# Two-block encoder on one core: moving operands of the split matmuls laid at set distances from the weight buffers, and attention matmuls on full 128x128 tiles

## The chip, the cores and the metric

The kernel runs on one core of a Trainium2 chip. The metric is the device time of one execution in microseconds (us): 1568.88 us before the change, the median of 3 runs (1568.62 to 1571.0).

## The reference

Two blocks run over 256 tokens of width 1024. The first puts 16 meta tokens ahead (272 rows) and has an even layer (latent attention and windowed attention, 8 heads each) and an odd layer (a linear recurrence). The second has two layers of FFN, hybrid mixer, FFN. What matters here, cut from the source:

```
# latent attention: the rotary key is one for all heads, 64 wide; scores over 128 + 64
k_pe = jnp.broadcast_to(k_pe[:, None], (B, MLA_HEADS, T, MLA_ROPE))
k = jnp.concatenate([k_nope, k_pe], axis=-1)
q = rms_norm(q, g_qn); k = rms_norm(k, g_kn)      # per head, over 192
o = blocked_dense_attention(q, k, v, MLA_QK ** -0.5)
...
def swiglu(x, w_gate, w_up, w_down):
    return (jax.nn.silu(x @ w_gate) * (x @ w_up)) @ w_down     # 1024 -> 2816 -> 1024
...
for l in range(DEPTH):
    x = x + 0.5 * swiglu(rmsnorm(x, ffn1_norm[l]), ffn1_w_gate[l], ffn1_w_up[l], ffn1_w_down[l])
    h = rmsnorm(x, mix_norm[l])
    x = x + hybrid_mixer(h, w_in[l], ...)          # 1024 -> 4608, a 4-head gated memory, 1024 -> 1024
    x = x + 0.5 * swiglu(rmsnorm(x, ffn2_norm[l]), ffn2_w_gate[l], ffn2_w_up[l], ffn2_w_down[l])
```

## The kernel before

Activations lie transposed: features on the 128 partitions, tokens along the free axis. A large product is exact to fp32 by parts: weight w and activation x are each cut into a high part in fp32r (ACT, a copy) and a low part (DVE, a subtraction), and `prod` (L437) issues three matmuls for each 128 x 128 piece of weight: hi with xh, hi with xl, lo with xh. The weight is the stationary operand, the activation the moving one, 272 columns in the even layer and the first half of the odd one, 256 in the rest. `mm3` (L453) does the same for operands that are given one by one, `split` (L464) cuts an activation into its two parts, and `feed` (L484) does so for the next stage's x.

Raw weights come by DMA on the SP queue into two buffers; pieces of 1024 columns are cut from them into 4 pairs of buffers, hi0 to hi3 and lo0 to lo3 (`cut`, L418). `more_cuts` (L1400) adds a fifth pair, hi4 and lo4, for the odd layer and all after it. A piece is released by the last matmul that reads it (`used`).

The order of instructions is made by a planner in `Builder`: each call runs a cost model of the engines (`Clock`, L118), `tick` (L324) resumes side work (norms, gates, attention heads, written as generators) when the model says that its inputs are there, and `pump` (L393) cuts the next piece of weight. All instructions go through one helper, so that the profile gives nearly all of them line 179.

The stages, by their time in the trace: the even layer to about 300 us, the odd layer to about 480, then for each of the two layers ffn1 (480 to 665, 1020 to 1207), hybrid (665 to 845, 1207 to 1390) and ffn2 (845 to 1020, 1390 to 1567).

- FFN (`ffn`, L1327): for each of 22 slices of 128 hidden features, gate and up take 2 x 8 x 3 matmuls over x's 8 parts of 128 features (x moving, 1056 in an FFN); down takes 8 x 22 x 3 = 528 with the hidden features ph/pl moving.
- Hybrid (`hybrid`, L1442): 768 matmuls with x as stated above (`pair`, L1465), 384 with the parts hh/hl, hph/hpl and mh/ml of later products moving. `memory` has a helper `small` (L1524) that issues 32 matmuls of 32 x 32 in two bursts with a yield between, six times a layer, and at its end spreads one row of scales over 128 partitions from tiles of 4 partitions (`spread`, L458).
- Odd layer: its output product moves oyh/oyl; there DVE runs the recurrence.
- Even layer: `rowsum` (L681) adds squares over partitions into row j of a bank by a matmul with a 128 x 32 window of constants, 28 times; `head` (L861) spreads a row of key scales (`rowkh`, `rowkl`, 32 partitions, times a column of the 32 x 32 identity `identr`) and makes the scores of a latent head from two products for each half of the queries: `mq` with `mk` over 128 features, and `mqr` with `kpe` over 64 partitions (two heads share a 128-partition tile of `mqr`). `query_scales` (L737), `window_scales` (L798) and `latent_scales` (L827) work on 32 rows; `shared_key` (L690) makes `kpe`.

x's parts xh and xl are tiles [128, 8, 272]. FFN and hybrid use `[:, k, :256]` of them, so that part k begins 1088 bytes behind part k-1.

Of the kernel before, what the change touches and what calls it, by code (L numbers as in the profile page):

```python
# [16 lines left out]
P = 128  # L17
# [24 lines left out]
_CST = (("ident", 128), ("ones", 128), ("row", 63), ("pair", 64), ("pe", 32), ("hsel", 128), ("dsel", 16))  # L42
# [13 lines left out]
C_AT, C_N = _offsets(_CST)  # L56
R_AT, R_N = _offsets(_ROT)
# [167 lines left out]
class Builder:  # L225

    AHEAD = 3

# [26 lines left out]
    def t(self, pool, shape, tag, dt=F32):  # L255
        tile_ = pool.tile(shape, dt, tag=tag, name=tag)
        self.clock.read[tile_.tensor.name] = [(0, 1 << 30, self.clock.at["pe"] + 0.3)]
        return tile_

# [198 lines left out]
    def spread(self, out, p, r, hi, lo):  # L458

        row = self.identr[0:p, r:r + 1].to_broadcast([p, P])  # L460
        self.mm(out=out, lhsT=row, rhs=hi, start=True, stop=False)
        self.mm(out=out, lhsT=row, rhs=lo, start=False, stop=True)
# [21 lines left out]
    def feed(self, gen, d, x, g, n):  # L484
        self.split(x, self.xh[:, d, :n], self.xl[:, d, :n], g)
        self.put("x", gen, d)
        self.spawn(self.square(gen, d, x, n))

# [53 lines left out]
    def first_norm(self):  # L542
        yield from self.until(self.clock.known(self.clock.wrote, self.cst.tensor.name))
        self.act(out=self.identr, in_=self.c("ident")[0:32, 0:32], func=AF.Copy)
# [18 lines left out]
    def setup(self):  # L563
# [7 lines left out]
        self.identr = self.t(self.const, [32, 32], "identr", F32R)  # L571
# [9 lines left out]
    def even(self):  # L581
# [152 lines left out]
        rowk = self.t(ev, [32, T], "rowk")  # L734
        rowkh, rowkl = self.t(ev, [32, T], "rowkh", F32R), self.t(ev, [32, T], "rowkl", F32R)

        def query_scales(rows, c0):  # L737
# [10 lines left out]
            tt(out=pk, in0=cp[:, 64:80], in1=self.c("dsel"), op=ALU.mult)  # L748
# [41 lines left out]
        r1 = self.t(ea, [32, T], "r1")  # L790
        qmr = self.t(ea, [P, 4, P], "qmr")
        sel = self.t(ea, [32, P], "sel")
# [5 lines left out]
        def window_scales():  # L798
# [4 lines left out]
            sd, r2 = yield from some(2)  # L803
            tt(out=r1, in0=rows[0:32, :T], in1=rb[0:32, :], op=ALU.mult)
            tt(out=r1, in0=r1, in1=rb[0:32, :], op=ALU.mult)
            yield
            yield from inverse(r1, 1.0 / P, sd[0:32, :], r2[0:32, :])
            stt(out=r1, in0=r2[0:32, :], scalar=float(P) ** -0.5, in1=rb[0:32, :], op0=ALU.mult, op1=ALU.mult)
# [4 lines left out]
            self.drop(sd, r2, rows)  # L813
# [13 lines left out]
        def latent_scales():  # L827
            rows = sums["lrows"]
            self.own(rows)
            sd, r2 = yield from some(2)  # L830
            yield from inverse(rows[0:32, :T], 1.0 / 192, sd[0:32, :], rowk)
# [4 lines left out]
            self.drop(sd, r2, rows)  # L836
# [24 lines left out]
        def head(h):  # L861
# [72 lines left out]
        def latent_query(h, ps):  # L934
# [392 lines left out]
    def ffn(self, name, layer, gen, nxt):  # L1327
# [114 lines left out]
    def hybrid(self, layer, gen):  # L1442
# [43 lines left out]
        def memory():  # L1486
# [37 lines left out]
            def small(i, ls, rs):  # L1524
                for h in range(H):
# [5 lines left out]
                    if h == 1:  # L1531
                        yield
# [20 lines left out]
            yield from small(0, kk_, qs)  # L1553
            inc, up = lf, None
            for i in range(8):
# [18 lines left out]
                if i < 5:  # L1574
                    yield from small(i + 1, kq, kq)
# [52 lines left out]
            rrh, rrl = hh[0:H, H - 1, :], hl[0:H, H - 1, :]  # L1628
            self.split(tp[0:H, 0:S], rrh, rrl)
# [233 lines left out]
def _layout(i):  # L1863
# [29 lines left out]
    for l in range(2):  # L1893
# [30 lines left out]
    row, pair, pe = (np.zeros((P, n), f32) for n in (63, 64, 32))  # L1924
    row[:, 31] = 1.0
    pair[:64, 31] = 1.0
    pair[64:, 32] = 1.0
    pe[:64, 8:16] = 1.0
# [3 lines left out]
        "ident": np.eye(P, dtype=f32), "ones": np.ones((P, P), f32), "row": row, "pair": pair, "pe": pe, "hsel": hsel,  # L1932
# [49 lines left out]
```

## Time and profile before

| what | value |
|---|---|
| median of 3 runs | 1568.88 us |
| profiled execution, its own time | 1568.53 us |
| its span, first to last instruction | 1566.7 us |
| PE busy in the span | 1546.1 us |
| DVE busy | 1116.8 us |
| ACT busy | 904.5 us |
| POOL busy | 24.1 us |
| mean granted TensorE clock | 0.999 |

Times of matmuls in a row overlap: a recorded duration includes the pipeline, and what one costs in a stream is the distance from its start to the next start. An fp32 matmul (not fp32r) leaves two records. The chain of waits follows the work that ended last backwards, so a long piece of it with one engine and a count gives the time of that many matmuls in a row. The view by stretch gives the busy time of every engine in a piece of the span.

### The profile page before, as it was taken

Reading aid. Unit: us, or ns where it says so; the run is one execution under the profiler, and the core shown is the slowest. Engines: PE = TensorE matmul, PEld = TensorE weight load, DVE = VectorE, ACT = ScalarE, POOL = GpSimd, SP = SyncE. Lnnn points to the kernel's source line nnn. Section 1 sums busy time; section 2 is a strip of 40 time slices with the busy share of each in tenths; the row PEclk is TensorE's granted clock in tenths of the full one; section 3 lists DMA queues with packets and bytes.
Section 4 is the critical chain, followed back from the end, with each engine's and each line's share of the span. In section 5 each row is a group of like instructions: output and inputs, shape, how many; then the busy total and the mean of one; then the engine's idle time right before and its main releaser. Section 6 shows DMA issues by size and latency. Waiting matters only on the chain.

```text
span 1566.7 us, 31037 instructions
## 1 busy us (share of the span) xinstructions
PE 1546.1 (99%) x12950; PEld 1484.6 (95%) x12950; DVE 1116.8 (71%) x1882; ACT 904.5 (58%) x1435; POOL 24.1 (2%) x58
## 2 busy tenths in 40 slices
PE   8999999999999999999999999999999999999998
PEld 8897679999989999999999999999999999999998
DVE  6877665679997666669776666666666698777754
ACT  7667544589966554475455544445444755555443
POOL 0000000000000000000000000000000000000000
PEclk9999999999999999999999999999999999999999
DMA  6422223554354555654445654655555543556553
GB/s 231 157 88 82 81 70 119 192 173 154 135 185 169 207 181 169 207 179 138 162 160 189 215 180 163 201 184 191 181 173 201 179 161 127 174 185 215 172 167 120
DMA packets 42492, 259.20 MB, mean 165 GB/s; under 512 B 4840, under 2 KB 6128, under 8 KB 18416
## 3 DMA queue, kind: packets, MB, share of 16 engines
q1 hardware_dynamic: 40624, 251.98, 46.6%
q10 hardware_dynamic: 1728, 5.24, 1.0%
q8 instruction: 101, 1.65, 0.4%
q14 instruction: 39, 0.32, 0.1%
HBM read 256.16 MB, written 1.05 MB: 164 GB/s over the span
## 4 chain that ended last, share of the span: by engine, by line
PE 90%; DVE 6%; ACT 2%; issue 1%; DMA 1%; POOL 0%; POOLq 0%; ACTq 0%; SPq 0%; DVEq 0%
PE acc L179 66%; PE m L179 24%; DVE lo L179 2%; DVE big L179 1%; ACT hi L179 1%; DVE kq L179 1%; DVE work L179 0%; DVE xx L179 0%; ACT st L179 0%; DMA raw<-in_hin_dram 0%; DVE st L179 0%; POOL col L179 0%; DMA raw<-in_first_dram 0%; DVE pr L179 0%; DVE xc L179 0%
## 5 line engine op out<-in xcount | busy, mean ns | idle before, releaser
L179 DVE TENSOR_TENSOR lo<-raw,hi 128x1024 fp32r<-128x1024 f32 (+3 forms) x520 | 582.3, 1129 | 263.0 <-ACT hi L179 248.5
L179 ACT ACTIVATE hi<-raw 128x1024 fp32r<-128x1024 f32 (+3 forms) x520 | 502.3, 979 | 323.5 <-PE acc L179 206.6
L179 PE MATMUL acc<-xh,hi 128*128 128x256 f32 (+1 forms) x2088 | 591.7, 283 | 5.6 <-ACT hi L179 5.6
L179 PE MATMUL acc<-xl,hi 128*128 128x256 f32 (+1 forms) x2088 | 594.6, 285 | 0.0
L179 PE MATMUL acc<-xh,lo 128*128 128x256 f32 (+1 forms) x2088 | 593.2, 284 | 0.0
L179 PEld LDWEIGHTS acc<-xh,hi 128*128 128x128 f32 x2088 | 394.7, 189 | 9.4 <-ACT hi L179 5.6
L179 PEld LDWEIGHTS acc<-xh,lo 128*128 128x128 f32 x2088 | 395.1, 189 | 2.7 <-issue 1.4
L179 PEld LDWEIGHTS acc<-xl,hi 128*128 128x128 f32 x2088 | 393.4, 188 | 2.3
L179 PE MATMUL acc<-ph,hi 128*128 128x256 f32 x704 | 196.8, 279 | 0.0
L179 PE MATMUL acc<-ph,lo 128*128 128x256 f32 x704 | 196.7, 279 | 0.0
L179 PE MATMUL acc<-pl,hi 128*128 128x256 f32 x704 | 196.7, 279 | 0.0
L179 PEld LDWEIGHTS acc<-pl,hi 128*128 128x128 f32 x704 | 132.4, 188 | 0.0
L179 PEld LDWEIGHTS acc<-ph,lo 128*128 128x128 f32 x704 | 132.3, 188 | 0.0
L179 PEld LDWEIGHTS acc<-ph,hi 128*128 128x128 f32 x704 | 132.3, 188 | 0.0
L179 PE MATMUL m<-xh,lo 128*128 128x256 f32 (+1 forms) x344 | 99.0, 288 | 0.0
L179 PE MATMUL m<-xh,hi 128*128 128x256 f32 (+1 forms) x344 | 98.7, 287 | 0.0
L179 PE MATMUL m<-xl,hi 128*128 128x256 f32 (+1 forms) x344 | 98.7, 287 | 0.0
L179 DVE TENSOR_TENSOR work<-acc,spread 128x256 f32<-128x256 f32 (+1 forms) x107 | 45.5, 426 | 46.6 <-PE acc L179 46.4
L179 ACT ACTIVATE work<-work 128x256 f32<-128x256 f32 (+2 forms) x92 | 37.4, 408 | 54.9 <-DVE work L179 54.5
L179 PEld LDWEIGHTS m<-xh,lo 128*128 128x128 f32 x344 | 65.4, 190 | 1.4 <-issue 0.9
L179 PEld LDWEIGHTS m<-xl,hi 128*128 128x128 f32 x344 | 65.4, 190 | 0.9 <-issue 0.9
L179 PEld LDWEIGHTS m<-xh,hi 128*128 128x128 f32 x344 | 65.4, 190 | 0.6 <-issue 0.4
(361 smaller groups left out, 2230.7 us busy)
## 6 DMA issues: line engine op xcount, KB each, us to landing
raw<-in_ffn_gu_dram SPq DMA_DIRECT2D x88, 1024.0 KB, 4.9
raw<-in_ffn_dn_dram SPq DMA_DIRECT2D x64, 704.0 KB, 4.1
raw<-in_hin_dram SPq DMA_DIRECT2D x32, 1024.0 KB, 4.9
raw<-in_oin_dram SPq DMA_DIRECT2D x16, 1024.0 KB, 4.9
raw<-in_ein_dram SPq DMA_DIRECT2D x12, 1024.0 KB, 4.7
raw<-in_eout_dram SPq DMA_DIRECT2D x8, 1024.0 KB, 4.9
raw<-in_oout_dram SPq DMA_DIRECT2D x8, 1024.0 KB, 5.0
raw<-in_wph_dram SPq DMA_DIRECT2D x8, 1024.0 KB, 4.8
```

What stands on the lines that cost most here:

```text
L179: r = f(*args, **kw)
```

## The change

1. **Where moving operands lie.** If n is 256, `feed` now writes x's parts to `sh` and `sl`: views of the same tiles from 128 bytes on, with the 8 parts of 256 columns one behind the other (step 1024 bytes). `ffn` and `hybrid` read these. `ffn` puts a gap of 160 bytes, `hybrid` one of 32, ahead of its tiles; the constants' tile has become 636 bytes shorter. By the two programs' allocations, the distance of a matmul's moving operand from its weight piece, in bytes modulo 256 (a weight piece's own address is 128 modulo 256, but for hi4 and lo4 before, which are 0):

| moving operand (256 columns) | matmuls | distance before | distance after |
|---|---|---|---|
| x in FFN and hybrid | 5760 | 0, 64, 128, 192 by part k | 192 |
| ph, pl of the FFN | 2112 | 32 (160 with hi4, lo4) | 64 |
| hh, hl, hph, hpl, mh, ml of the hybrid | 768 | 32 (160 with hi4, lo4) | 192 |
| oyh, oyl of the odd layer | 384 | 64 (192 with hi4, lo4) | 192 |
| x in the odd layer's gate | 384 | 0, 64, 128, 192 | 0, 64, 128, 192 |

Operands of 272 columns keep all four distances.

2. **Full tiles.** Constants for `rowsum` come from a 405 column tile `pick` that POOL fills, and are 128 x 128 windows. `kpe` is copied by POOL into `kz`, one slice for even heads with the lower half zero and one for odd heads with the upper half zero, so that the score products take 128 partitions. `rowk`, `rowkh`, `rowkl`, `sel`, `kpe_sq`, `identr` have 128 partitions, and `query_scales` transposes 128 x 128 blocks. At the hybrid's end, `rc` is a zeroed tile of 256 columns, so that transposes and spreads are 128 x 128 too.

3. **`small`** has no yield within: its two bursts of 16 become one of 32.

The diff, cut to its core:

```diff
     AHEAD = 3
+    X_AT = 32
+    gaps = 0
...
+    def gap(self, pool, n):
+
+        if n:
+            self.gaps += 1
+            pool.tile([P, n // 4], F32, tag=f"gap{self.gaps}", name=f"gap{self.gaps}")
...
-    def spread(self, out, p, r, hi, lo):
-
-        row = self.identr[0:p, r:r + 1].to_broadcast([p, P])
+    def spread(self, out, r, hi, lo):
+
+        row = self.identr[:, r:r + 1].to_broadcast([P, P])
         self.mm(out=out, lhsT=row, rhs=hi, start=True, stop=False)
         self.mm(out=out, lhsT=row, rhs=lo, start=False, stop=True)
...
     def feed(self, gen, d, x, g, n):
-        self.split(x, self.xh[:, d, :n], self.xl[:, d, :n], g)
+        if n == S:
+            self.place(gen)
+            self.split(x, self.sh[:, d, :], self.sl[:, d, :], g)
+        else:
+            self.split(x, self.xh[:, d, :n], self.xl[:, d, :n], g)
         self.put("x", gen, d)
         self.spawn(self.square(gen, d, x, n))
+
+    def place(self, gen):
+
+        at = self.X_AT
+        self.sh, self.sl = [t.rearrange("p k t -> p (k t)")[:, at:at + KD * S].rearrange("p (k t) -> p k t", t=S) for t in (self.xh, self.xl)]
...
-        def rowsum(bank, sq, lhsT, first, last, p=P):
-            mm(out=bank[0:32, :T], lhsT=lhsT, rhs=sq[0:p, :], start=first, stop=last)
-
-        row = lambda j: self.c("row")[:, 31 - j:63 - j]
-        pair = lambda j: self.c("pair")[:, 31 - j:63 - j]
+        def rowsum(bank, sq, lhsT, first, last):
+            mm(out=bank[:, :T], lhsT=lhsT, rhs=sq, start=first, stop=last)
+
+        pick = self.t(ea, [P, S_N], "pick")
+        at = {n: a_ for n, (a_, w) in S_AT.items()}
+        nc.gpsimd.memset(pick, 0.0)
+        nc.gpsimd.memset(pick[:, at["row"] + 15:at["row"] + 16], 1.0)
+        nc.gpsimd.memset(pick[0:64, at["pair"] + 6:at["pair"] + 7], 1.0)
+        nc.gpsimd.memset(pick[64:128, at["pair"] + 7:at["pair"] + 8], 1.0)
+        nc.gpsimd.memset(pick[0:64, at["pe"] + 8:at["pe"] + 16], 1.0)
+        row = lambda j: pick[:, at["row"] + 15 - j:at["row"] + 143 - j]
+        pair = lambda j: pick[:, at["pair"] + 6 - j:at["pair"] + 134 - j]
 
         kpe = self.t(ev, [P, T], "kpe")
-        kpe_sq = self.t(ea, [64, T], "kpe_sq")
+        kz = self.t(ev, [P, 2, T], "kz")
+        nc.gpsimd.memset(kz, 0.0)
+        kpe_sq = self.t(ea, [P, T], "kpe_sq")
...
-            act(out=kpe_sq, in_=z[0:64, :], func=AF.Square)
+            act(out=kpe_sq, in_=z, func=AF.Square)
             yield from rope(z, "mla", self.v("mk_rope"), self.v("mk_swap"), kpe, 32, sw, t1)
+            for i in range(2):
+                nc.gpsimd.tensor_copy(out=kz[64 * i:64 * i + 64, i, :], in_=kpe[64 * i:64 * i + 64, :])
 
...
-        rowk = self.t(ev, [32, T], "rowk")
-        rowkh, rowkl = self.t(ev, [32, T], "rowkh", F32R), self.t(ev, [32, T], "rowkl", F32R)
+        rowk = self.t(ev, [P, T], "rowk")
+        rowkh, rowkl = self.t(ev, [P, T], "rowkh", F32R), self.t(ev, [P, T], "rowkl", F32R)
...
-                nc.tensor.transpose(cp[:, j * 32:j * 32 + 32], rows[0:32, NM + j * P:NM + (j + 1) * P], ident[0:32, 0:32])
-            mm(out=cp[:, 64:80], lhsT=self.c("hsel")[0:32, :], rhs=rows[0:32, 0:NM], start=True, stop=True)
-            yield
-            cv = cp[:, 0:64].rearrange("p (j r) -> p j r", j=2)[:, :, 0:8]
+                nc.tensor.transpose(cp[:, j * P:j * P + P], rows[:, NM + j * P:NM + (j + 1) * P], ident)
+            mm(out=cp[:, 256:272], lhsT=self.c("hsel"), rhs=rows[:, 0:NM], start=True, stop=True)
...
-                self.spread(bp[:, :T], 32, 8 + h, rowkh, rowkl)
+                self.spread(bp[:, :T], 8 + h, rowkh, rowkl)
...
-                    p0 = 64 * (h % 2)
                     mm(out=ps[:, :T], lhsT=mq[:, h, qs], rhs=mk[:, h, :], start=True, stop=False)
-                    mm(out=ps[:, :T], lhsT=mqr[p0:p0 + 64, h // 2, qs], rhs=kpe[p0:p0 + 64, :], start=False, stop=True)
+                    mm(out=ps[:, :T], lhsT=mqr[:, h // 2, qs], rhs=kz[:, h % 2, :], start=False, stop=True)
...
-                rowsum(sums["lrows"], kpe_sq, self.c("pe")[0:64, :], True, False, 64)
+                rowsum(sums["lrows"], kpe_sq, pick[:, at["pe"]:at["pe"] + P], True, False)
...
-        x, xh, xl = self.x, self.xh, self.xl
+        x, xh, xl = self.x, self.sh, self.sl
         cols = slice(0, S)
         rh = self.rh
+        self.gap(ff, 160)
         ph = self.t(ff, [P, KFF, S], "ph", F32R)
         pl = self.t(ff, [P, KFF, S], "pl", F32R)
...
         self.phase(gen)
         hy = self.pool(st, "hy")
+        self.gap(hy, 32)
         self.make(hy, "kq", 2, [P, H, S])
-        x, xh, xl = self.x, self.xh, self.xl
...
                         mm(out=lv[i // 2][p0:p0 + 32, c0:c0 + 32], lhsT=ls[:, h, s0], rhs=rs[:, h, s0], start=True, stop=True)
-                    if h == 1:
-                        yield
+
...
-            yield from small(0, kk_, qs)
+            small(0, kk_, qs)
+            yield
...
-                    yield from small(i + 1, kq, kq)
+                    small(i + 1, kq, kq)
...
-            var, rc = [t[:, 0:8] for t in (yield from self.grab("mx", 2))]
+            var = (yield from self.grab("mx"))[:, 0:8]
+            rc = (yield from self.grab("work"))[:, 0:2 * P]
+            nc.gpsimd.memset(rc, 0.0)
...
-            nc.gpsimd.tensor_tensor(out=rc, in0=var, in1=self.half, op=ALU.pow)
+            byj = lambda t: t.rearrange("p (j c) -> p j c", j=2)[:, :, 0:H]
+            nc.gpsimd.tensor_tensor(out=byj(rc), in0=byj(var), in1=byj(self.half), op=ALU.pow)
...
-                nc.tensor.transpose(tp[0:H, j * P:(j + 1) * P], rc[:, j * H:(j + 1) * H], ident)
...
+                nc.tensor.transpose(tp[:, j * P:(j + 1) * P], rc[:, j * P:(j + 1) * P], ident)
...
-                    self.spread(ps[:, g * S:(g + 1) * S], H, 2 * i + g, rrh, rrl)
+                    self.spread(ps[:, g * S:(g + 1) * S], 2 * i + g, rrh, rrl)
```

What the change does to the order on PE, at three places. In the order's rows a line stands for one instruction (or for several equal ones, x16), output and operands by name, with the number of a buffer behind it.

A row sum in the even layer, between products with x; `work_83` holds squares, `cst` the constants, `m_71` the bank of sums. Before:

```order
L179 MATMUL m_68<-xl,hi_76 128x272
L179 MATMUL m_68<-xh,lo_80 128x272
L179 MATMUL m_71<-work_83,cst 32x272
L179 MATMUL m_68<-xh,hi_76 128x272
L179 MATMUL m_68<-xl,hi_76 128x272
```

Now:

```order
L181 MATMUL m_70<-xl,hi_76 128x272
L181 MATMUL m_70<-xh,lo_80 128x272
L181 MATMUL m_71<-work_83,pick 128x272
L181 MATMUL m_70<-xh,hi_76 128x272
L181 MATMUL m_70<-xl,hi_76 128x272
```

The place in the order is the same; the row sum takes its window from `pick` and writes 128 rows in place of 32.

The spread and the scores of latent head 0, `m_70` (now `m_71`) being the spread's bank, the two others those of the scores. Before:

```order
L179 MATMUL m_70<-rowkh,identr 128x272
L179 MATMUL m_70<-rowkl,identr 128x272
L179 MATMUL acc_64<-xh,hi_74 128x272
L179 MATMUL acc_64<-xl,hi_74 128x272
L179 MATMUL m_66<-sq_t,mq 128x272
L179 MATMUL m_66<-kpe,mqr 128x272
L179 MATMUL m_69<-sq_t,mq 128x272
L179 MATMUL m_69<-kpe,mqr 128x272
```

Now:

```order
L181 MATMUL m_71<-rowkh,identr 128x272
L181 MATMUL m_71<-rowkl,identr 128x272
L181 MATMUL acc_64<-xh,hi_74 128x272
L181 MATMUL acc_64<-xl,hi_74 128x272
L181 MATMUL m_69<-sq_t,mq 128x272
L181 MATMUL m_69<-kz,mqr 128x272
L181 MATMUL m_66<-sq_t,mq 128x272
L181 MATMUL m_66<-kz,mqr 128x272
```

The order is the same again; the rotary part reads `kz` in place of `kpe`, and `rowkh`, `rowkl` and `identr` have 128 partitions.

The first level of `memory`'s small matmuls, hybrid of the first layer (`kq_6486`, now `kq_6497`, is the tile that both operands come from). Before:

```order
L179 MATMUL acc_65<-xl,hi_75 128x256
L179 MATMUL m_68<-kq_6486 32x32 x16
L179 MATMUL acc_65<-xh,lo_79 128x256
L179 MATMUL acc_65<-xh,hi_76 128x256
L179 MATMUL acc_65<-xl,hi_76 128x256
L179 MATMUL m_68<-kq_6486 32x32 x16
L179 MATMUL acc_65<-xh,lo_80 128x256
L179 MATMUL acc_65<-xh,hi_76 128x256
```

Now:

```order
L181 MATMUL acc_65<-xl,hi_75 128x256
L181 MATMUL acc_65<-xh,lo_79 128x256
L181 MATMUL m_67<-kq_6497 32x32 x32
L181 MATMUL acc_65<-xh,hi_75 128x256
L181 MATMUL acc_65<-xl,hi_75 128x256
L181 MATMUL acc_65<-xh,lo_79 128x256
```

The second burst of 16 has joined the first. PE has 11,666 rows in place of 11,678: of the 24 bursts 12 have gone.

## Rows read from the trace of the kernel before

**Rows 1.** The page: busy time, share and instructions of each engine; the chain's shares.

```profile
PE 1546.1 (99%) x12950; PEld 1484.6 (95%) x12950; DVE 1116.8 (71%) x1882; ACT 904.5 (58%) x1435; POOL 24.1 (2%) x58
...
PE 90%; DVE 6%; ACT 2%; issue 1%; DMA 1%; POOL 0%; POOLq 0%; ACTq 0%; SPq 0%; DVEq 0%
```

**Rows 2.** By stretch: length, busy us of engines, granted clock, DMA share, GB/s.

```profile
30.00:84.00 54.00, 54.00 (x385) 48.30 (x384) 46.53 (x76) 37.19 (x68) 0.00 (x0) 1.00 0.38 134
...
150.00:250.00 100.00, 100.00 (x545) 74.58 (x544) 64.01 (x168) 54.86 (x123) 0.00 (x0) 1.00 0.19 68
...
345.00:480.00 135.00, 129.53 (x990) 124.55 (x989) 132.23 (x188) 112.95 (x189) 0.00 (x0) 1.00 0.48 164
...
480.00:615.00 135.00, 135.00 (x1146) 135.00 (x1146) 85.03 (x143) 75.36 (x108) 0.70 (x1) 1.00 0.52 179
```

**Rows 3.** Chain of waits in ffn2, layer 0, gate and up: start, us, count.

```profile
854.92 90.16 PE acc L179 x763
```

**Rows 4.** Chain of waits in ffn1, layer 0, down.

```profile
605.99 54.11 PE acc L179 x462
```

**Rows 5.** Chain of waits in the odd layer's output product, two stretches.

```profile
420.84 13.20 PE m L179 x112
...
463.50 9.52 PE m L179 x84
```

**Rows 6.** Timeline of PE, odd output product, after a stall: start, us, operation.

```profile
447.79 0.39 PE L179 MATMUL m<-oyh,lo 128*128 128x256 f32 x1 [1.60 <-DVE lo L179]
448.01 0.28 PE L179 MATMUL m<-oyh,hi 128*128 128x256 f32 x1
...
451.31 0.28 PE L179 MATMUL m<-oyl,hi 128*128 128x256 f32 x1
```

**Rows 7.** Timeline of PE: a row sum of 128 x 32 between products with x.

```profile
60.07 0.28 PE L179 MATMUL m<-xl,hi 128*128 128x272 f32 x1
60.28 0.65 PE L179 MATMUL m<-work,cst 128*32 128x272 f32 x2
60.85 0.39 PE L179 MATMUL m<-xh,lo 128*128 128x272 f32 x1
61.08 0.29 PE L179 MATMUL m<-xh,hi 128*128 128x272 f32 x1
```

**Rows 8.** Timeline of PE: a product with squares on a full tile.

```profile
71.31 0.28 PE L179 MATMUL m<-hi,xl 128*96 128x256 f32 x1
71.43 0.62 PE L179 MATMUL m<-work,cst 128*128 128x272 f32 x2
71.69 0.48 PE L179 MATMUL m<-hi,xh 128*96 128x256 f32 x1
72.01 0.28 PE L179 MATMUL m<-lo,xh 128*96 128x256 f32 x1
```

**Rows 9.** Timeline of PE: spread, a value product, the scores of latent heads.

```profile
212.84 0.29 PE L179 MATMUL acc<-xh,hi 128*128 128x272 f32 x1
213.06 0.39 PE L179 MATMUL m<-rowkh,identr 32*128 32x272 f32 x1
...
213.73 1.54 PE L179 MATMUL m<-pt,vv 96*128 96x272 f32 x6
215.10 0.62 PE L179 MATMUL m<-sq_t,mq 128*128 128x272 f32 x2
...
217.85 0.29 PE L179 MATMUL acc<-xh,hi 128*128 128x272 f32 x1
```

**Rows 10.** Timeline of PE, hybrid: first and last row around two spreads.

```profile
757.27 0.28 PE L179 MATMUL acc<-xh,lo 128*128 128x256 f32 x1
...
758.37 0.28 PE L179 MATMUL acc<-xl,hi 128*128 128x256 f32 x1
```

**Rows 11.** The tile kpe: durations min/median/max in ns, first and last start.

```profile
L179 PE MATMUL m<-kpe,mqr x32: 389/441/493, 182.5 to 240.3; 64*128 64x272 f32 x32
L179 DVE TENSOR_TENSOR kpe<-work,work x1: 444/444/444, 37.7 to 37.7; 128x272 f32<-128x272 f32 x1
```

More of the change, by code (lines that the diff above doesn't have):

```diff
@@ L41 @@
 )
-_CST = (("ident", 128), ("ones", 128), ("row", 63), ("pair", 64), ("pe", 32), ("hsel", 128), ("dsel", 16))
+_CST = (("ident", 128), ("ones", 128), ("hsel", 128), ("dsel", 16))
+_SEL = (("row", 143), ("pair", 134), ("pe", 128))
 _ROT = (("swa_c", T), ("swa_s", T), ("mla_c", T), ("mla_s", T))
@@ L56 @@
 C_AT, C_N = _offsets(_CST)
+S_AT, S_N = _offsets(_SEL)
 R_AT, R_N = _offsets(_ROT)
@@ L543, in first_norm @@
         yield from self.until(self.clock.known(self.clock.wrote, self.cst.tensor.name))
-        self.act(out=self.identr, in_=self.c("ident")[0:32, 0:32], func=AF.Copy)
+        self.act(out=self.identr, in_=self.c("ident")[:, 0:32], func=AF.Copy)
         yield from self.norm(0, T, (0, P, 2 * P, 0, 96, 176))
@@ L570, in setup @@
         self.rt = self.t(self.const, [P, 2], "rt")
-        self.identr = self.t(self.const, [32, 32], "identr", F32R)
+        self.identr = self.t(self.const, [P, 32], "identr", F32R)
         self.x = self.t(self.const, [P, KD, T], "x")
@@ L741, in query_scales @@
             for j in range(2):
-                nc.tensor.transpose(cp[:, j * 32:j * 32 + 32], rows[0:32, NM + j * P:NM + (j + 1) * P], ident[0:32, 0:32])
-            mm(out=cp[:, 64:80], lhsT=self.c("hsel")[0:32, :], rhs=rows[0:32, 0:NM], start=True, stop=True)
+                nc.tensor.transpose(cp[:, j * P:j * P + P], rows[:, NM + j * P:NM + (j + 1) * P], ident)
+            mm(out=cp[:, 256:272], lhsT=self.c("hsel"), rhs=rows[:, 0:NM], start=True, stop=True)
             yield
-            cv = cp[:, 0:64].rearrange("p (j r) -> p j r", j=2)[:, :, 0:8]
+            cv = cp[:, 0:256].rearrange("p (j r) -> p j r", j=2)[:, :, 0:8]
             nc.scalar.copy(out=qc[:, 0:2, c0:c0 + 8], in_=cv)
             act(out=nqc[:, 0:2, c0:c0 + 8], in_=cv, func=AF.Copy, scale=-1.0)
-            tt(out=pk, in0=cp[:, 64:80], in1=self.c("dsel"), op=ALU.mult)
+            tt(out=pk, in0=cp[:, 256:272], in1=self.c("dsel"), op=ALU.mult)
             nc.vector.tensor_reduce(out=qc[:, 2, c0:c0 + 1], in_=pk, axis=AX.X, op=ALU.add)
@@ L789, in even @@
         qm = self.t(ea, [P, 8 * 144], "qm")
-        r1 = self.t(ea, [32, T], "r1")
         qmr = self.t(ea, [P, 4, P], "qmr")
-        sel = self.t(ea, [32, P], "sel")
+        sel = self.t(ea, [P, P], "sel")
         def meta_rows(src):
@@ L802, in window_scales @@
             nc.gpsimd.memset(qm, 0.0)
-            sd, r2 = yield from some(2)
-            tt(out=r1, in0=rows[0:32, :T], in1=rb[0:32, :], op=ALU.mult)
-            tt(out=r1, in0=r1, in1=rb[0:32, :], op=ALU.mult)
+            sd, r2, r1 = yield from some(3)
+            tt(out=r1, in0=rows[:, :T], in1=rb, op=ALU.mult)
+            tt(out=r1, in0=r1, in1=rb, op=ALU.mult)
             yield
-            yield from inverse(r1, 1.0 / P, sd[0:32, :], r2[0:32, :])
-            stt(out=r1, in0=r2[0:32, :], scalar=float(P) ** -0.5, in1=rb[0:32, :], op0=ALU.mult, op1=ALU.mult)
+            yield from inverse(r1, 1.0 / P, sd, r2)
+            stt(out=r1, in0=r2, scalar=float(P) ** -0.5, in1=rb, op0=ALU.mult, op1=ALU.mult)
             yield
@@ L812, in window_scales @@
             ts(out=nsink, in0=self.vec[:, at:at + 9], scalar1=-1.0, scalar2=None, op0=ALU.mult)
-            self.drop(sd, r2, rows)
+            self.drop(sd, r2, r1, rows)
             meta_rows(sq_t)
@@ L829, in latent_scales @@
             self.own(rows)
-            sd, r2 = yield from some(2)
-            yield from inverse(rows[0:32, :T], 1.0 / 192, sd[0:32, :], rowk)
+            sd, r1 = yield from some(2)
+            yield from inverse(rows[:, :T], 1.0 / 192, sd, rowk)
             ts(out=r1, in0=rowk, scalar1=192.0 ** -0.5, scalar2=None, op0=ALU.mult)
@@ L835, in latent_scales @@
             yield from query_scales(r1, 0)
-            self.drop(sd, r2, rows)
+            self.drop(sd, r1, rows)
             meta_rows(mq)
@@ L1450, in hybrid @@
         hy = self.pool(st, "hy")
+        self.gap(hy, 32)
         self.make(hy, "kq", 2, [P, H, S])
-        x, xh, xl = self.x, self.xh, self.xl
+        x, xh, xl = self.x, self.sh, self.sl
         cols = slice(0, S)
@@ L1625, in memory @@
             for j in range(2):
-                nc.tensor.transpose(tp[0:H, j * P:(j + 1) * P], rc[:, j * H:(j + 1) * H], ident)
+                nc.tensor.transpose(tp[:, j * P:(j + 1) * P], rc[:, j * P:(j + 1) * P], ident)
             yield
-            rrh, rrl = hh[0:H, H - 1, :], hl[0:H, H - 1, :]
-            self.split(tp[0:H, 0:S], rrh, rrl)
+            rrh, rrl = hh[:, H - 1, :], hl[:, H - 1, :]
+            self.split(tp[:, 0:S], rrh, rrl)
             yield
@@ L1923, in _layout @@
     p = np.arange(P)
[L1924 to L1928, printed above, removed]
     hsel = np.zeros((P, P), f32)
@@ L1931, in _layout @@
     cst = {
-        "ident": np.eye(P, dtype=f32), "ones": np.ones((P, P), f32), "row": row, "pair": pair, "pe": pe, "hsel": hsel,
+        "ident": np.eye(P, dtype=f32), "ones": np.ones((P, P), f32), "hsel": hsel,
         "dsel": (p[:, None] % NM == np.arange(NM)[None, :]).astype(f32),
```

## The prediction

> **What bounds the kernel.** I read the page first. It shows PE busy 1546.1 of 1566.7 us and 90% of the chain of waits on PE [rows 1]: the time is the number of matmuls times the distance from one start to the next, and little else. The profiled execution took 1568.5 us, 0.3 us under the median of 1568.9, so the sum is made against 1568.5. The view by stretch tells where this holds without reserve. In 480 to 615 us PE is busy all of 135.00 us and DVE 85.03, at a granted clock of 1.00 and a DMA share of 0.52, so a faster PE finds its weights ready; only in 345 to 480 us does DVE work 132.23 of 135 us and set the pace [rows 2]. The third view, long pieces of the chain, gives the price of one matmul of 256 columns where nothing interrupts it. With x moving it is 90.16 us / 763 = 118.17 ns [rows 3], with ph and pl 54.11 / 462 = 117.12 ns [rows 4].
>
> The row that decides this prediction is another one. In the odd layer's output product the same instruction, at the same clock, goes at 13.20 / 112 = 117.86 ns in one stretch and at 9.52 / 84 = 113.33 ns in another [rows 5]. Both are long runs that neither start nor end in a stall, so each is a beat that holds itself: below, the short beat (113.33) and the long beat (117.86). By the allocations this is the one product before whose moving operand lies at 64 or 192 from its weights, and it is at those distances that the change puts FFN and hybrid. Nowhere in x's stream (all four distances in turn) or in ph's (32 and 160) does the chain show a piece at 113 ns.
>
> **The change, part by part.**
>
> *x at distance 192.* Gate and up are 4 x 1056 = 4224 matmuls; each saves 118.17 - 113.33 = 4.84 ns if the short beat is held, in all 20.4 us. The hybrid's 1536 with x: 7.4 us. Bounds: nothing, if the long beat of 117.86 ns is held (it would give 0.3 ns each, 1.8 us over 5760), and 27.8 us.
>
> *ph, pl at 64, the hybrid's own parts at 192.* 2112 x (117.12 - 113.33 = 3.79 ns) = 8.0 us, and 768 x 3.79 = 2.9 us, since those parts lie at ph's distances now. At 117.86 ns they would lose 0.7 ns each, 2.1 us.
>
> For all four the ceiling is 38.7 us. Which of the two will be held? Against the short one: after a stall of 1.60 us on DVE the output product, at distance 64, starts at 447.79 us and then runs (451.31 - 448.01) / 28 = 117.9 ns [rows 6], the long beat. For it: the short stretch was entered where, in a running stream, the weights went from hi0 to hi4 and so the distance from 64 to 192, and it outlived the changes of buffer after that [rows 5]. The changed kernel crosses between 64 and 192 in the same way at each step from down to the next stage's x and from gate and up to down, and an FFN has no stall in which PE would have to start anew (135.00 of 135.00 us busy [rows 2]). In a hybrid, small matmuls break the stream dozens of times and each return is a new start. So I take the FFN's part whole (28.4 us) and half of the hybrid's (5.2 of 10.3): **33.6 us**.
>
> *The odd layer.* Its output product goes to 192 for every weight buffer; DVE sets the pace there [rows 2], and whatever PE gains is waited away. Zero; at most 384 x 4.5 ns = 1.7 us.
>
> *Full tiles in the even layer.* A row sum on a 128 x 32 tile, from the product ahead of it to the second one behind, takes 61.08 - 60.07 = 1.01 us [rows 7]. Two of the three intervals in it that would be there anyway are ordinary ones of 0.126 us, so 0.76 us is its price. On a full tile the same sequence is 72.01 - 71.31 = 0.70 us, less 2 x 0.118 is 0.46 [rows 8]. 28 x 0.30 = 8.4 us. The scores of a latent head take 217.85 - 215.10 = 2.75 us, with four changes between 128 and 64 partitions [rows 9]. A row of equal fp32 products costs (215.10 - 213.73) / 6 = 0.229 us a record [rows 9]; eight records of that and one ordinary interval are 1.96 us. 8 heads x 0.79 = 6.3 us. The spread: 213.73 - 212.84 = 0.89 us for four intervals [rows 9] that would be 0.51 at 0.126; 8 x 0.38 = 3.0 us. I put the four transposes of `query_scales` (32 columns before, 128 now) at nothing: 96 columns more at 0.229 us for 272 are 0.08 us each, and the changes of shape around them go in return.
>
> *Hybrid, spreads and bursts.* Four pairs of spreads: 758.37 - 757.27 = 1.10 us for six intervals [rows 10] that would be 0.70; 4 x 0.40 = 1.6 us. A burst of 32 x 32 tiles is entered and left with the same change of shape; from 212.84 to 213.06 us such a change costs 0.22 - 0.126 = 0.09 us [rows 9]. 12 bursts go, with two changes each: between 0 (if a longer burst waits for DVE longer) and 2.2 us, I take half.
>
> These are 8.4 + 6.3 + 3.0 + 1.6 + 1.1 = 20.4 us of PE time. Not all lies on the path. In 30 to 84 us DVE works 46.53 of 54 us, in 150 to 250 us 64.01 of 100 [rows 2], while PE is never idle in either; 90% of the chain is PE [rows 1]. I take 17, between 13 and 20.4.
>
> *What is added.* POOL fills `pick` and `kz` at the start, copies `kpe` into `kz`, and zeroes `rc` twice. POOL is busy 24.1 us of the span [rows 1]. `kpe` is written at 37.7 us and first read by a score at 182.5 [rows 11], so 145 us hide the two copies; were they late, head 0 would wait, not PE, which has the gates' products to go on with. `rc`'s memset comes before the `var` it waits for, so that it lies beside that product. The queue on SP gets no new transfer; the constants' one is 636 bytes per partition shorter. ACT and DVE work on 128 rows instead of 32 with the same number of columns, which I price at nothing.
>
> **Sum:** 1568.5 - 33.6 - 17 = 1517.9, so **1518 us**. For this case alone: down to 1508 (38.7 and 20.4 + 1.5 of the odd layer and the bursts), up to 1530 (gate and up alone at the short beat, with 5 of the rest, and 13 from the tiles).
>
> **The rivals.**
>
> *Part of it only.* PE falls back into the long beat at places in the FFN too, and stays there until something disturbs it. For it: the restart at distance 64 gave the long beat [rows 6]. Half of the 33.6 us gives 1568.5 - 16.8 - 17 = 1535, from 1530 to 1545.
>
> *The distances are worth nothing.* The long beat, 117.86 ns, stands everywhere: 5760 x 0.3 less 2880 x 0.7 is 0, and 1568.5 - 17 is about 1552, from 1548 to 1556. For it speaks every long-beat stretch of the output product at these same distances [rows 5, 6]. Against it stands the short stretch beside it, 4.5 ns a matmul quicker at the same clock [rows 5], so that something besides columns and clock does set the interval; the rival gets less than a quarter.
>
> The Trainium skill speaks for this rival: "SBUF — State Buffer", section "Who interferes with whom", gives PE two read ports, one for the moving operand and one for the weight load, that are independent of each other, and says that PE never waits on anyone. By it an address would change nothing, and the time would be that 1552. The trace does not agree: one instruction has two levels there, 117.86 and 113.33 ns [rows 5].
>
> *A third, worse beat.* One distance for all k may lock the stream where the four distances in turn wandered. 8640 matmuls (4224 + 2112 + 1536 + 768) have their place at stake, at a mean of 117.8 ns now. If the lock costs over 17 us / 8640 = 2.0 ns, that is from 119.8 ns on, the tiles' gain is gone and the kernel is slower than before. One step of the 4.5 ns between the two known beats [rows 5] above 117.86 would be 122.4: 8640 x 4.6 = 40 us, 1568.5 - 17 + 40 = about 1591. Nothing in the trace shows such an interval in a stream.
>
> *The change doesn't do what it says.* The full tiles' gain is waited away by DVE in the even layer, and the distances are worth nothing: about 1567. Against it: PE is busy 100.00 of 100.00 us while DVE is busy 64.01 [rows 2].
>
> **How the numbers follow.** My forecast 0.50, part only 0.20, nothing from the distances 0.24, a worse beat 0.04, no effect at all 0.02. The first two hold 0.70, so the range reaches over the third: 1508 to 1556, which leaves out the last two and some tails, not over 0.15. For this kernel 0.2%, 3 us, is about what a measurement can tell from no change. Faster by more than that: 0.94 (the first three); within: 0.02; slower: 0.04.
>
> **What would show it.** In the chain of the changed kernel, gate and up's long pieces at 113 to 114 ns a matmul (right), at 118 (the third case), in pieces of both (the second). The mean recorded duration of the FFN's 256-column forms would fall with it. A row sum's neighbours should lie 0.30 us closer, a latent head's scores should take 1.96 us, and PE's idle time should stay where it is. The forecast is wrong if gate and up do not go below 117 ns, or if they do and DVE or the weights' DMA then ends PE's waits in the FFN.

## The result, and the profile after

The changed kernel takes 1542.59 us, the median of 4 runs (1540.02 to 1542.7), against 1568.75 us before: a ratio of 0.9825 (0.9811 to 0.984). The time lies in the range, and within the band of the prediction's second case (1530 to 1545): 26 us were won where 51 were forecast. The profiled execution took 1542.62 us, with a span of 1540.5.

Busy times and chain shares on the page of the changed kernel:

```profile
PE 1507.8 (98%) x12950; PEld 1473.7 (96%) x12950; DVE 1115.9 (72%) x1882; ACT 904.9 (59%) x1435; POOL 26.2 (2%) x68
...
PE 63%; issue 19%; DVE 10%; ACT 5%; DMA 2%; POOL 0%; POOLq 0%; ACTq 0%; SPq 0%; DVEq 0%
```

Against [rows 1], PE's busy time fell by 38 us, the span by 26: PE idles 32.7 us now, where it idled 20.6. Part of what was won is waited away.

The chain of waits of the changed kernel, one long piece for gate and up of the first FFN, its down, and gate and up of the second, third and fourth FFN (start, us, count):

```profile
524.92 50.09 PE acc L181 x442
...
584.99 50.05 PE acc L181 x425
...
844.95 80.09 PE acc L181 x680
...
1019.90 90.21 PE acc L181 x796
...
1420.86 44.20 PE acc L181 x390
```

They answer to [rows 3, 4]. Per matmul: 113.33, 117.76, 117.78, 113.33 and 113.33 ns. These pieces have the two beats of [rows 5] and no other, the short one to a hundredth of a nanosecond, the long one within a tenth: the pieces of three gate-and-ups hold the short one, that of the second the long one. Down holds the long one, in all four FFNs (the other three by their starts: 117.78).

The second FFN did not begin in the long beat. In each gate and up the norm puts two groups of small fp32 matmuls into the stream. The timeline of PE shows them in the first FFN and in the second:

```profile
465.63 0.50 PE L181 MATMUL m<-cst,acc 128*128 128x1 f32 x4
...
466.19 0.28 PE L181 MATMUL m<-xh,lo 128*128 128x256 f32 x1
...
467.96 0.28 PE L181 MATMUL m<-xh,lo 128*128 128x256 f32 x1
468.08 0.61 PE L181 MATMUL m<-work,cst 128*128 128x128 f32 x4
...
814.00 0.61 PE L181 MATMUL m<-cst,acc 128*128 128x1 f32 x4 [0.69 <-DVE acc L181]
...
819.39 0.71 PE L181 MATMUL m<-work,cst 128*128 128x128 f32 x4
```

In both FFNs the stream was short up to the first group and long behind it: (467.96 - 466.19) / 15 = 118.0 ns in the first FFN, where PE had not waited at all. Behind the second group it was short again in the first FFN, and stayed long in the second.

The timeline of PE, a row sum and the scores of the first latent head:

```profile
61.13 0.29 PE L181 MATMUL acc<-xh,lo 128*128 128x272 f32 x1
61.26 0.62 PE L181 MATMUL m<-work,pick 128*128 128x272 f32 x2
61.52 0.49 PE L181 MATMUL acc<-xh,hi 128*128 128x272 f32 x1
61.85 0.29 PE L181 MATMUL acc<-xl,hi 128*128 128x272 f32 x1
...
175.95 0.62 PE L181 MATMUL m<-sq_t,mq 128*128 128x272 f32 x2
...
177.91 0.29 PE L181 MATMUL acc<-xh,hi 128*128 128x272 f32 x1
```

The row sum with its neighbours takes 61.85 - 61.13 = 0.72 us where it took 1.01 [rows 7], the scores 1.96 us where they took 2.75 [rows 9]. ffn1 of the first layer begins at 458.0 us in place of 473.0.

PE's waits that have grown, in the changed kernel (what it waited for: us in total, times, longest):

```profile
PE m L181 <- DVE kq L181: 6.4, 12, 0.9
...
PE m L181 <- DVE pt L181: 3.1, 2, 1.9
PE m L181 <- DVE xx L181: 1.9, 1, 1.9
PE acc L181 <- DVE hpl L181: 1.2, 1, 1.2
```

Before, `kq` stood at 1.3 us and `pt` at 0.2; `xx` and `hpl` did not occur. `kq` is the tile of the hybrids' small matmuls, `pt` that of an attention head's probabilities. The last two are one place in the second hybrid, shown by the timeline of PE:

```profile
1297.58 0.38 PE L181 MATMUL acc<-hpl,hi 128*128 128x256 f32 x1 [1.17 <-DVE hpl L181]
...
1299.97 1.22 PE L181 MATMUL m<-xx,pw 128*128 128x256 f32 x2 [1.90 <-DVE xx L181]
1301.76 0.58 PE L181 MATMUL acc<-hph,hi 128*128 128x256 f32 x1 [0.56 <-ACT hph L181]
```

The product of the pooled branch with its weights is reached before that branch is made. And the view by stretch (columns as in [rows 2]) shows what such idling costs beyond itself:

```profile
100.00:110.00 10.00, 8.08 (x41) 6.80 (x41) 6.71 (x24) 6.23 (x19) 0.00 (x0) 0.91 0.00 0
...
1290.00:1300.00 10.00, 6.93 (x57) 6.38 (x55) 8.50 (x20) 3.90 (x6) 1.12 (x1) 0.97 0.31 107
1300.00:1310.00 10.00, 9.44 (x53) 8.48 (x54) 4.12 (x7) 6.90 (x8) 0.00 (x0) 0.69 0.12 27
```

After PE was busy only 6.93 of 10 us, the granted clock of the next 10 us is 0.69 on the mean, so that part of them went at the lower of the two levels; the second hybrid takes 173.2 us in place of 167.6. After the wait of 1.92 us for `pt` near 105 us it is 0.91.

### The profile page after: what moved, and what is told of

Its sections match the earlier page's. It is cut to its first block, busy times and chain, and to the rows that moved or that the text cites. A ratio compares the mean times of both kernels' runs of the same rounds, so it can differ in the third digit from the quotient of the medians.

```text
span 1540.5 us, 31049 instructions
## 1 busy us (share of the span) xinstructions
PE 1507.8 (98%) x12950; PEld 1473.7 (96%) x12950; DVE 1115.9 (72%) x1882; ACT 904.9 (59%) x1435; POOL 26.2 (2%) x68
## 4 chain that ended last, share of the span: by engine, by line
PE 63%; issue 19%; DVE 10%; ACT 5%; DMA 2%; POOL 0%; POOLq 0%; ACTq 0%; SPq 0%; DVEq 0%
PE acc L181 51%; PE m L181 12%; DVE lo L181 4%; DVE big L181 3%; ACT hi L181 2%; DMA raw<-in_hin_dram 1%; ACT L181 1%; DVE kq L181 1%; ACT big L181 1%; ACT w L181 0%; DVE xc L181 0%; ACT xx L181 0%; DVE xx L181 0%; DMA raw<-in_ffn_gu_dram 0%; DVE work L181 0%
## 5 line engine op out<-in xcount | busy, mean ns | idle before, releaser
L181 PE MATMUL m<-xl,hi 128*128 128x256 f32 (+1 forms) x336 | 95.6, 284 | 0.0
L181 PE MATMUL m<-xh,hi 128*128 128x256 f32 (+1 forms) x336 | 95.5, 284 | 0.0
```

Source lines behind the costliest of these rows:

```text
L181: r = f(*args, **kw)
```

## The experiments

**Which half of the change gives what.** Two kernels separate them. The first is the kernel before with the new places alone (with 128 bytes of padding that stand for the shorter constants):

```diff
+        if n == S:
+            self.place(gen)
+            self.split(x, self.sh[:, d, :], self.sl[:, d, :], g)
...
+        self.gap(ff, 160)
...
+        self.gap(hy, 32)
```

> The kernel before with only the new places of the moving operands (all distances as in the changed kernel), its narrow tiles and its two bursts kept. Theory: the distances give what the change of interval times the count gives in the changed kernel's trace, some 15 us in gate and up, 5 in the hybrid's products with x, 1 in its other parts, less 2 in down: about 19 us, 1549 us, and no long waits of PE in the hybrid. Rival: part of this is waited away on DVE as soon as PE is faster, whatever the tiles: PE's idle time grows by 5 us or more and the time is 1554 us or more.

Measured: 1546.12 us, a ratio of 0.9856 (0.984 to 0.9873) to the kernel before on the same chip, 22 us won. Its first FFN's chain, gate and up, then down:

```profile
516.80 68.23 PE acc L179 x602
...
594.97 55.12 PE acc L179 x468
```

That is 113.34 and 117.78 ns. All four gate-and-ups held the short beat here, which explains 3 us more than expected; the waits for `kq` were 2.6 us. So the distances alone do what their intervals say, and cost hardly any waits.

The second is the changed kernel with x's parts, gaps and weight buffers at the places of before:

```diff
-        self.gap(ff, 160)
+        self.gap(ff, 0)
...
-        self.gap(hy, 32)
+        self.gap(hy, 0)
...
+        self.sh, self.sl = self.xh[:, :, :S], self.xl[:, :, :S]
```

> The changed kernel with x's parts, gaps and weight buffers back at the places of before, so that only full tiles and the single burst stand. Theory: the tiles give 13 us or more up to the odd layer's end as forecast, and the hybrids are no slower than before: 1551 to 1556 us. Rival: the stalls of the changed kernel (on DVE's kq in both hybrids, on hpl in the second) come from the new order and not from the faster stream; then they stand here too, about 10 us, and the time is 1560 us or more.

Measured: 1559.16 us, ratio 0.994 (0.9925 to 0.9955), at the edge of the rival. ffn1 began at 457.8 us, as in the changed kernel, so the tiles give their 15 us ahead of it. Then 6 are lost again: PE waits 4.1 us for `kq`, 1.1 for `hpl` and 1.9 for `xx` in this kernel too, and the second hybrid takes 173.3 us. The stall belongs to the tiles' half of the change.

**The single burst.** In two kernels the yield within `small` was put back, once in the changed kernel and once in the one with tiles alone:

```diff
+                    if h == 1:
+                        yield
...
-            small(0, kk_, qs)
-            yield
+            yield from small(0, kk_, qs)
...
-                    small(i + 1, kq, kq)
+                    yield from small(i + 1, kq, kq)
```

> The changed kernel with the yield within the small matmuls put back, so that 16 and 16 are issued in two bursts. Theory: the single burst is what waits for DVE's kq (6.4 us of PE's waits after, 1.3 before), for it is issued whole as soon as the planner believes kq ready; with two bursts the waits fall to 2 us or less and the hybrids gain 3 to 5 us against 2 us for twelve changes of shape: 1539 to 1541 us. Rival: the faster stream brings PE to kq too early, in one burst or two: the waits stay above 5 us and the time is 1543 to 1545 us.

> The run with full tiles alone (1559.2 us), its single burst of small matmuls made two again. Theory: the single burst is what took back the tiles' gain in the second hybrid (wait for hpl, then a lower granted clock); without it the tiles stand as forecast, 13 to 17 us below the kernel before: 1552 to 1555 us. Rival: the stalls are those of the new order as such: 1558 to 1560 us.

Measured: 1539.28 us (ratio 0.9811, 0.9797 to 0.9826), 3.3 us under the changed kernel, and 1553.39 us (0.9901, 0.9888 to 0.9915), 5.8 us under the tiles alone. With the new distances the ratios' intervals of one and two bursts overlap (0.9811 to 0.984 for one), with the old ones they do not. The stages say the same in both: the second hybrid takes 166.7 us in place of 173.2 with the new distances, 168.1 in place of 173.3 with the old ones. With the new distances the first hybrid takes 2.4 us longer, 165.0 in place of 162.6: its own parts went at 117.78 ns in this run, at 113.33 in the changed kernel's. The waits in the first of the two kernels:

```profile
PE m L181 <- DVE pt L181: 3.1, 2, 1.9
PE m L181 <- DVE kq L181: 2.0, 6, 1.0
```

`kq` is back at 2.0 us, `hpl` and `xx` are gone from the list, and the granted clock of 1300 to 1330 us is 1.00 in both kernels. The waits for `pt` in the even layer stayed, 3.1 us; they come with the tiles, and no run tried to take them away. With two bursts the full tiles alone give 15 us, inside the 13 to 20.4 of the prediction: without the new distances the single burst took back 6.

**What holds a beat.** Down was moved to distance 192, like x:

```diff
-        self.gap(ff, 160)
+        self.gap(ff, 32)
```

> The changed kernel with the FFN's gap 32 in place of 160 bytes, so that ph and pl lie at distance 192 like x, in place of 64; nothing else. Theory A: a stream at 64 or 192 keeps the beat that it was entered with, and the crossing from 192 to 64 puts it into the long one. Then down keeps the beat of gate and up: 113.3 ns where those have it, 117.8 ns only behind a gate and up at 117.8. Three of four FFNs gain 528 x 4.45 ns, 7 us: about 1535 us. Rival B: distance 64 itself goes with the long beat and 192 with the short one: all four downs at 113.3, 9.4 us, about 1533. Rival C: the product with ph is bound to the long beat by something else than its distance: down stays at 117.8 and the time at 1542.6.

Measured: 1536.42 us, ratio 0.9784 (0.9754 to 0.9814), single runs from 1527.38 to 1538.15. The interval overlaps that of the changed kernel (0.9811 to 0.984); what the edit does is read from the trace. The chain: down of the first FFN; gate and up of the second; gate and up, then down, of the fourth:

```profile
584.99 50.09 PE acc L181 x442
...
829.95 90.10 PE acc L181 x795
...
1411.96 43.11 PE acc L181 x366
1469.91 50.17 PE acc L181 x426
```

113.33 ns in the first two rows, 117.79 and 117.77 in the last two. In three FFNs gate, up and down are short throughout, in the fourth all are long: down has no beat of its own, it keeps the one that it is entered with. Theory A stands for distance 192, and rivals B and C fall. That single runs differ by 11 us fits with a beat that is drawn anew in each run; it is not shown, since the beats of each kernel are read from one profiled execution.

Then all operands of FFN and hybrid went to one other distance, 64 or 0:

```diff
-    X_AT = 32
+    X_AT = 64
...
-        self.gap(ff, 32)
+        self.gap(ff, 160)
...
-        self.gap(hy, 32)
+        self.gap(hy, 160)
```

(48, 96 and 96 for distance 0.)

> As the run with down at 192, but x, ph, pl and the hybrid's parts all at distance 64. Theory: what puts a stream out of the short beat is the crossing from 192 to 64, not the distance 64: with one distance throughout, gate, up and down of an FFN have one beat, 113.3 in some FFNs, and the time is 1530 to 1545 us. Rival: 64 goes with the long beat: 117.8 ns in gate, up and down everywhere, some 25 us more than with 192, about 1560 us.

> As the run with down at 192, but x, ph, pl and the hybrid's parts all at distance 0. Theory: 64 and 192 are the ones that can hold 113.3 ns; at 0 nothing in the trace of before holds a beat under 116, and gate and up take 117 ns or more: 1557 us or more. Rival: one distance for all is what counts, whichever: 113.3 ns in most FFNs and 1530 to 1545 us.

Measured: 1560.67 us (0.9947, 0.9932 to 0.9962) and 1577.46 us (1.0058, 1.0043 to 1.0073). The chain of the first FFN, gate and up and then down, at distance 64:

```profile
505.59 74.44 PE acc L181 x632
...
589.92 50.17 PE acc L181 x426
```

and at distance 0:

```profile
505.51 74.52 PE acc L181 x621
...
589.99 50.04 PE acc L181 x417
```

117.78 and 117.77 ns at 64; 120.00 and 120.00 at 0. All four FFNs are like the first in both kernels. The theory for 64 falls: 64 goes with the long beat in the FFNs, and no small matmul of the norm brought a stream back to the short one there, as happened at 192 (in the third FFN of the changed kernel, at 1000.8 us). In the hybrids, stretches of x at 64 did go at 113.33 ns, up to 87 matmuls in a row. At 0 there is a third beat, of 120.00 ns, and with it the kernel is slower than before: the mechanism of the prediction's third rival exists, at a distance that the change does not use.

Last, the crossing turned round: x at 64, down at 192.

```diff
-    X_AT = 32
+    X_AT = 64
```

(from the kernel with down at 192)

> As the run with down at 192, but x at distance 64 in FFN and hybrid: the crossings of the changed kernel the other way round. Theory: a crossing from 64 at the long beat to 192 gives the short one, one from 192 at the short beat to 64 gives the long one; then gate and up run mostly at 117.8 and all four downs at 113.3, against three FFNs whole at 113.3: 14 us lost in gate and up, 2 won in down, some 3 lost in the hybrids, about 1551 us. Rival: the beat is kept over crossings and drawn by what comes before: gate, up and down of an FFN agree, 1530 to 1545 us.

Measured: 1552.49 us, ratio 0.9899 (0.9883 to 0.9916). The chain: gate and up, then down of the first FFN; down of the second; down of the third:

```profile
504.48 75.61 PE acc L181 x642
...
589.98 50.09 PE acc L181 x442
...
939.95 50.06 PE acc L181 x425
...
1124.92 50.17 PE acc L181 x426
```

117.77, 113.33, 117.79 and 117.77 ns. Gate and up were long in all four, down short in the first and the fourth and long in the second and third. So the theory holds for gate and up, and for two of the four downs. Over the traces of the changed kernel, of the distances alone and of the two bursts, a short stream at 192 became long on entering 64 in 10 of 10 cases, and a long one at 64 became short on entering 192 in 8 of 9. In this last trace it was 4 of 4 for the first kind, and 3 of 5 for the second (the four downs and the first hybrid's own parts).

All these crossings were made by the moving operand: in these kernels every weight buffer lies at 128 modulo 256, so that the distance and the operand's own address cannot be told apart. Before the change hi4 and lo4 lay at 0, and the odd layer's output product, whose operand keeps its address, crosses there by the weights alone. By the program's order of weight buffers, the short stretch of [rows 5] from 463.50 us on goes from 192 to 64 three times, the last 54 matmuls all at 64, and holds 113.33 ns; the long stretch beside it has 24 matmuls at 192 from 428.81 us, at 117.96. The two kernels with the tiles alone, whose weights lie as before, kept 113.33 ns over the same three crossings. A change of distance that the weights make did not put a stream out of the short beat, then; what counts may be the operand's own address, and no run separates the two in FFN or hybrid.

**A better version.** First, 192 throughout and two bursts together, the edits of the two runs above in one kernel:

```diff
-        self.gap(ff, 160)
+        self.gap(ff, 32)
...
+                    if h == 1:
+                        yield
```

> Both edits together: ph and pl at distance 192, and the two bursts of small matmuls put back. Theory: they act in different places (down, and the hybrids' waits), so that their gains add: 6 us of the one and 3 to 6 of the other, 1530 to 1533 us, with no wait for hpl in the second hybrid. Rival: which beat a stage gets is drawn anew by every change of what comes before it, and more FFNs fall into the long one: 1536 us or more.

Measured: 1529.83 us, ratio 0.9747 (0.9726 to 0.9768), at the lower end of the theory, with one FFN of four mostly in the long beat. The timeline of PE within gate and up of its first FFN, and the chain ahead of that place and behind it:

```profile
540.98 0.28 PE L181 MATMUL acc<-xh,lo 128*128 128x256 f32 x1
541.59 0.36 PE L181 MATMUL acc<-xh,hi 128*128 128x256 f32 x1 [0.33 <-DVE work L181]
541.79 0.28 PE L181 MATMUL acc<-xl,hi 128*128 128x256 f32 x1
...
503.18 31.85 PE acc L181 x281
...
544.89 95.17 PE acc L181 x808
```

31.85 / 281 = 113.35 ns ahead, 95.17 / 808 = 117.78 ns behind, through the rest of gate and up and the whole of down: a wait of a third of a microsecond, with no other matmul in between, was followed by another beat for some 860 matmuls. So I let the stream cross once in each product: the last of x's eight parts lies 64 or 128 bytes further, at distance 0 or 64.

```diff
+        ats = [at + d * S + (16 if d == KD - 1 else 0) for d in range(KD)]
```

(32 for the second.)

> As the run with 192 throughout and two bursts (1529.8 us), but the last of x's eight parts lies 64 bytes further, at distance 0, so that every product of eight parts comes back from 0 to 192 once. In the trace of before 37 of 48 such returns ended in the short beat. Theory: the return draws the stream into the short beat within a product or two, so that no FFN stays in the long one and down enters in the short one: gate and up at about 114.2 ns (3 of 24 matmuls at up to 120), all downs at 113.3; the hybrids' own parts too: 1523 to 1528 us. Rival: the excursion throws a stream out of the short beat as often as it brings it in: gate and up alternate, 116 ns or more on the mean, 1536 us or more.

> The same with the last part at distance 64. Theory, from the crossings after down (long at 64 to short at 192 in 7 of 8): it works too but costs more, as each return shows 117, 116 and 116 before 113: gate and up at 114.4 to 115 ns, 1526 to 1532 us. Rival: three matmuls at 64 are too few to reach the phase from which that crossing leads to the short beat: gate and up at 116 ns or more, 1538 us or more.

Measured: 1525.8 us (0.973, 0.9717 to 0.9743), the lowest of all, and 1533.78 us (0.9773, 0.9756 to 0.9789). The chain with the last part at 0, gate and up, then down of the first FFN:

```profile
503.38 71.71 PE acc L181 x628
...
584.98 50.09 PE acc L181 x442
```

114.19 and 113.33 ns, alike in all four FFNs, and the hybrids' own parts at 113.4 and 113.6, as the theory had it: no FFN stays in the long beat any more, at a price of 0.9 ns in gate and up. Against 1529.83 us the gain is not clear, for the two kernels' intervals overlap. With the last part at 64 the time lies between theory and rival: the second FFN stayed long throughout, and the hybrids' own parts went at 117.77 ns. Three matmuls there do not always bring the stream back.

## Why the prediction was right, and where its sum was off

The range held the time, and the direction was right; the sum was 25 us too good. The range held because it had been stretched over the third case; the forecast itself, the whole of the FFN's part, did not come.

- **x at 192** was forecast at 20.4 us in gate and up. Three FFNs took the short beat to the hundredth (113.33), the second the long one: about 15 us. The prediction put nothing into an FFN from which PE would start anew. There are the norm's small matmuls: the second FFN left the short beat at the first group, behind a wait of 0.69 us for DVE's `acc` at 814.0 us, and was long from there on. That the wait did it is not shown: the first FFN changed its beat at the same place without a wait, and in the kernel with the distances alone a wait of 0.96 us there was followed by a return at the second group. A wait by itself was followed by such a switch in the run with two bursts at 192. In the hybrids x went at 114.3 to 115.4 ns on the mean where 118 stood, 5.4 us for 3.7.
- **ph, pl at 64** is the step that failed: "I take the FFN's part whole" priced down at 113.33 and 8.0 us, with the argument that the changed kernel crosses between 64 and 192 "in the same way" as the short stretch of [rows 5] had. It does not: there the weights made the crossing and the operand kept its address, here the operand makes it. From 192 to 64 it led into the long beat in 14 of 14 cases, back into the short one in 11 of 14. Down went from 117.12 to 117.78 ns and lost 1.5 us; the bound that the prediction had named, 0.7 ns lost, was the value.
- **The hybrid's own parts**: short in the first, long in the second, 1.2 us of the 1.5 forecast. In all the distances took some 20 us off the matmuls' intervals in place of 33.6.
- **Full tiles in the even layer** were right in size and place: 0.29 us a row sum (0.30 forecast), 0.79 us a head's scores (0.79), 15.0 us on the start of ffn1. The spreads' part was not read by itself.
- **Hybrid, spreads and bursts** had the wrong sign. 2.7 us of gain were priced, and a longer wait on DVE only as something that would bring the bursts' gain down to 0. With the single burst PE came to `kq` and to the pooled branch too early, and with the lower granted clock behind it this cost 6 us where the distances were the old ones. With the new ones the second hybrid takes 173.2 us, as with tiles alone (173.3): what x gained in it, some 3 us, is gone again, and the waits for `kq` (6.4 us against 4.1) make it likely that they took it. The spreads' 1.6 us are not seen: with two bursts and old distances the two hybrids take 334.5 us together, before 334.7. PE's idle time, which the prediction named as a sign, did not stay where it was.
- **What was added** did not hold up PE at `kz`: its copies stand at 36.9 and 37.5 us, `kz` is first read at 176.

The rivals: "part of it only" was nearest, at 1535 us, though for another reason than given, the move from x's place to that of ph and pl rather than restarts alone. "The distances are worth nothing" would have been the time of the tiles with two bursts, 1553.39 us. The rule of the Trainium skill that speaks for it ("SBUF — State Buffer", section "Who interferes with whom": the moving operand and the weight load have independent ports, and PE waits on no one), as the prediction reads it, does not agree with these runs: addresses alone move a matmul from 113.33 to 120.00 ns and the kernel from 1536.42 to 1577.46 us. What it is in the machine that makes the beats, no run here shows.

## What to carry to other kernels

If a stream of equal matmuls on one engine bounds a kernel, divide long pieces of the chain by their counts: two sharp values at one clock mean that something other than columns sets the interval, and operands' addresses are worth a try, one place modulo 256 bytes for every product of the stream and not a different one for each. Which place counts too: of the three tried here 192 gave 1536.42 us, 64 gave 1560.67 and 0 gave 1577.46, against some 1559 with the old places; the others were not tried. A gain of this kind depends on how the stream was entered, so count it by stages, and look for short waits and for small matmuls of another kind at the point where a stage changes its value. Before a row of the old kernel is taken as a model, ask what made the change in it: there it was the weights' address, in the new kernel the operand's. When bursts of small work are merged, ask what it waits for: here the merged burst met 6.4 us of waits for `kq`, two bursts 2.0.

## What the runs showed of the hardware that was not expected

At a granted clock of 1.00, a matmul of 256 columns whose moving operand keeps one distance from its weights (modulo 256 bytes, the weights at 128) held one of three intervals here: 113.33 or 117.78 ns at 192, 117.78 at 64 in every FFN, 120.00 at 0. At 192 it kept either value over changes of weight buffer, product and stage, through whole FFNs of 1584 matmuls. It changed at a wait of 0.33 us, at small fp32 matmuls in the stream without any wait (from 113.33 to 118.0 ns and back in the first FFN), or where the operand moved from 192 to 64. Where the weights made that crossing, in the odd layer before, 113.33 ns stayed. And two waits of 1 to 2 us in a row were followed by a mean granted clock of 0.69 over the next 10 us.
